# A split written into earlier products, two differences put first, and a second bank for the prompt's products, in an encoder layer on one core

## Chip, core and metric

The kernel runs on one core of a Trainium2 chip, as one launch. The metric is the device time of that core in microseconds (us). The core has five engines that run side by side, each working off its own instructions in order: TensorE (PE in the profile, its weight loads PEld) multiplies matrices into eight banks of PSUM, VectorE (DVE) and ScalarE (ACT) do the elementwise work, GpSimd (POOL) a part of it, and SyncE (SP) issues most DMAs. Engines wait for each other by semaphores.

## The reference

One encoder layer over two inputs: a sample of 1024 tokens and a prompt of 256, with a width of 1024, all in float32. Cut to what matters here:

```
h = rmsnorm(x, g_mix);  z = h @ w_in                       # queries, keys, values, gates
o_a = banded attention (8 heads);  o_b = dilated mixture (12 heads, merged to 4)
merged = gate_a * (o_a @ w_branch_a) + gate_b * (o_b @ w_branch_b)
x = x + merged @ w_out                                     # the output projection
h = rmsnorm(x, g_mlp)
x = x + square(relu(h @ w_up)) @ w_down                    # 1024 -> 4096 -> 1024
y = rmsnorm(x, g_final)
```

## The kernel before

**Products in parts.** A float32 product is made of three products of rounded numbers. Each operand is split into a high half (a copy to a rounded type, ScalarE, L185 in `split`) and a low half (the difference from it, VectorE, L186). One step in the contraction dimension is then three matmuls: high with low, low with high, high with high (`mm3` for the branches and the output projection, `six` for what follows). So each product waits for two operands that two engines make, one behind the other.

**Order of the stages.** The 1280 tokens are ten tiles of 128, in three blocks: 512 and 512 of the sample, 256 of the prompt (`BLOCKS`). After attention come the branch products (the loop over `jobs`, 48 products of 128 output columns each): for each block the eight of branch b and the first four of branch a, and after these, for each of the three blocks, the last four of branch a. A product's bank is multiplied by its gate (L1484) and added to `mT`, the merged rows turned over, one tile of `mT` for two or four column groups (L1485, both on VectorE). The last four products, of the 256-token block, are 256 wide; the eight ahead of them 512. The banks tagged "mm", three of them, are taken in turn.

Then comes the output projection, twice over all ten tiles, `hh` = 0 and 1 for the two halves of the output columns. `part(t)` splits a tile's merged rows: four copies and four low halves, two column groups each, into `mhi` and `mlo`; tile t + 2 is split after tile t's product. In the first half the result is added to the residual rows `x2` (L1599), which DMAs from SP bring (L1492). In the second half each tile is added (L1608), normed, turned over on TensorE (L340) and copied out (L1522, L1505), and the combinations for the next stage are made in between.

**Who sets the order.** From the end of attention to the end of the first half of the output projection a planner orders the instructions of each engine: it goes through the stretch with costs of its own and gives each engine the first instruction in the program that is ready. The place in the program is the priority. Most tiles there (`mT`, `x2`, `mhi`, `mlo`, gates, operands of the branches) come from one pool of 33 buffers of 4 KB a partition (`slot`). From the second half on (`manual_schedule` at L1579) each engine runs in the order of the program text.

**The up product.** It multiplies the sample's normed rows, as a 2 x 2 matrix of blocks, with the weights in Strassen's manner: seven block products instead of eight, named A11, A12, S2, S3, S1, A22, S4, with sums of blocks as operands. `combine` makes these sums (L1532 to L1537); `combine_last` makes the last of them, S4's operand, in two tiles, each a difference (L1545, in place) and its split. `up(j)` runs once for each of 16 pairs of column groups: the seven products into the banks x, y ("mm" and "pt") and z ("sc"), which add up over several products, so that a bank must be read before the next product adds to it. After S1, for instance, L1853 reads x on VectorE, and S4 adds to x later. The prompt's 256 rows are multiplied without the scheme, two products of 24 matmuls for a pair (`prompt(parts[0])` and `prompt(parts[3])`, L349), both in the one bank tagged "pv"; `prompt_out` reads such a bank on ScalarE (L1849 and L1850, relu and square, for both halves). In pair 0 the two stand next to each other, and pair 1's first follows at once; in the later pairs the first stands after A12, the second at the end. "sc" has two banks; z takes one for each pair, and in pair 0 the transposes of the last tile (`turn_prompt(9, ("pt", "sc"))`) the other.

Pair 0 takes extra steps between its products from `entering` in the last function: splits of S3, S1 and A22, `combine_last` after S3's product, `split_prompt` after A22's; and the first two products of pair 1 stand ahead of S4's. The operands of pair 1 are made on VectorE (L391, L314, L316); GpSimd adds the finished columns (L1925 to L1928), and SP stores them (L1930).

The down product that follows (`Down`) takes all eight banks in turn.

Of the kernel before, what the change touches and what calls it, by code (L numbers as in the profile page):

```python
# [11 lines left out]
F32R = mybir.dt.float32r  # L12
# [3 lines left out]
P = 128  # L16
D = 1024
KC = D // P
NS, NP = 1024, 256
T = NS + NP  # L20
NT = T // P
# [76 lines left out]
def encoder_kernel(  # L98
# [28 lines left out]
    def slot(name, shape=(P, D), dt=F32):  # L127
        return slots.tile(list(shape), dt, name=name, tag="m", bufs=N_M)
# [4 lines left out]
    def qslot(name, shape, dt=F32):  # L133
        return narrows[0].tile(list(shape), dt, name=name, tag="q", bufs=N_Q)

    def bank(tag, name=None):
        return psum.tile([P, 512], F32, name=name or tag, tag=tag, bufs={"mm": 3, "sc": 2, "pt": 2, "pv": 1}[tag])
# [46 lines left out]
    def split(hi, lo, src):  # L184
        nc.scalar.activation(hi, src, AF.Copy)  # L185
        nc.vector.tensor_tensor(lo, src, hi.bitcast(F32), op=ALU.subtract)  # L186
# [9 lines left out]
    def run(gen):  # L196
        for _ in gen:
            pass
# [146 lines left out]
    def six(ps, lefts, rights, first, last, mid=None):  # L345

        seq = [x for (lh, ll), (rh, rl) in zip(lefts, rights) for x in ((rl, lh), (rh, ll), (rh, lh))]
        for i, (a, b) in enumerate(seq):
            nc.tensor.matmul(ps, a, b, start=first and i == 0, stop=last and i == len(seq) - 1,  # L349
                             skip_group_check=True)  # L350
            if mid and i == len(seq) // 2 - 1:
                mid()

    def each(part, sub):
        hi, lo = part
        if sub is None:
            return [(hi[:, k, :], lo[:, k, :]) for k in range(KC)]
        if len(hi.shape) == 4:
            return [(hi[:, sub, k, :], lo[:, sub, k, :]) for k in range(4)]
        return [(hi[:, 4 * sub + k, :], lo[:, 4 * sub + k, :]) for k in range(4)]  # L360
# [4 lines left out]
    def prompt(part, tag="pv", mid=None):  # L365

        ps = bank(tag)
        lefts = [(hp[k // 4][0][:, k % 4, :], hp[k // 4][1][:, k % 4, :]) for k in range(KC)]
        six(ps[:, :NP], lefts, each(part, None), True, True, mid)
        return ps  # L370
# [937 lines left out]


    mT = Wide("mT", KC, F32, ())  # L1310
    if True:
        ob_hi, ob_lo = Wide("obhi", 2, F32R, ()), Wide("oblo", 2, F32R, ())
        o_hi, o_lo = Wide("ohi", 4, F32R, ()), Wide("olo", 4, F32R, ())
# [52 lines left out]
        n = len(order)  # L1366
# [49 lines left out]
        jobs = [(x, b, c) for b in range(3) for x in "ba" for c in range(KC if x == "b" else 4)]  # L1416
# [41 lines left out]
        for i, (x, b, c) in enumerate(jobs):  # L1458
            t0, n = BLOCKS[b]
            load_gate(i + 6)  # L1460
            if i in (0, 1, 2, 3, 8, 9):
                load_o(i + 4 if i < 4 else i)
            for f, t in side.get(i, ()):
                f(t)
            open_gate(i + 3)
            if i in (1, 4, 22, 26):
                fetch()
            elif i in (5, 8, 33, 35):
                w_as[(5, 8, 33, 35).index(i)] = weight(0)
            elif i in (38, 40, 42, 44):  # L1470
                prepare()
            hi, lo = w_bs[c // 4] if x == "b" else w_as[c // 2]
            per, src = (4, (ob_hi, ob_lo)) if x == "b" else (2, (o_hi, o_lo))
            cols = slice(P * (c % per), P * (c % per) + P)
            ps = bank("mm")
            run(mm3(ps[:, :n], [((hi[:, k, cols], lo[:, k, cols]), tuple(y.at(k, t0, n) for y in src))
                                for k in range(2 if x == "b" else 4)]))
            if (b, 0) not in mT.t:
                mT.block(b)
            m, sg = mT.at(c, t0, n), sgs.pop(i)  # L1480
            if x == "b":
                nc.vector.tensor_tensor(m, ps[:, :n], sg, op=ALU.mult)
            else:
                nc.vector.tensor_tensor(sg, ps[:, :n], sg, op=ALU.mult)  # L1484
                nc.vector.tensor_tensor(m, m, sg, op=ALU.add)  # L1485

    att_pool.close()

# [53 lines left out]
    def combine_last():  # L1542
        s2, a12 = combined[S2], combined[S4]
        for i in range(2):
            nc.vector.tensor_tensor(a12[i], a12[i], s2[i], op=ALU.subtract)  # L1545
            act[S4][i] = slot("chi", (P, 2, 512), F32R), slot("clo", (P, 2, 512), F32R)
            split(*act[S4][i], a12[i])

# [3 lines left out]
    with ExitStack() as pre:  # L1552
        late = pre.enter_context(tc.tile_pool(name="late", bufs=4))

        def lslot(name, shape=(P, D), dt=F32):
            return late.tile(list(shape), dt, name=name, tag="l4", bufs=6)

        for i in (4, 5, 6):
            specs[n_out + i] = specs[n_out + i][:2] + (lslot,)
        gm = slot("gm2")  # L1560
        nc.sync.dma_start(gm, g_mlp[0].partition_broadcast(P))
        xn = {}
        p0 = []
        b0 = right_up(0, p0, slot)

        def ahead():

            yield from b0
            yield from halves(A11, raws_h[0, 0])
            yield from halves(A12, raws_h[0, 1])  # L1570

        more, sums = ahead(), combine()
        for hh in range(2):
            sl = slice(512 * hh, 512 * hh + 512)
            ws = [weight(0) for _ in range(4)]
            parts = {}
            if hh:

                ctx.enter_context(tc.manual_schedule(engines=ALL))  # L1579

            def part(t):
                if t >= NT:
                    return
                n = 2 if hh else KC
                mhi = [qslot("mhi", (P, n, P), F32R) if hh else slot("mhi", (P, n, P), F32R) for _ in range(KC // n)]
                mlo = slot("mlo", (P, KC, P), F32R)
                for c in range(0, KC, 2):
                    split(mhi[c // n][:, c % n : c % n + 2, :], mlo[:, c : c + 2, :], mT.at(c, P * t, P, 2))
                parts[t] = [(mhi[k // n][:, k % n, :], mlo[:, k, :]) for k in range(KC)]

            part(0)
            part(1)
            for t in range(NT):
                m = parts.pop(t)
                ps = bank("mm")
                run(mm3(ps, [(m[k], (ws[k // 2][0][:, k % 2, :], ws[k // 2][1][:, k % 2, :]))
                             for k in range(KC)]))
                if hh == 0:
                    nc.vector.tensor_tensor(x2[t][:, sl], x2[t][:, sl], ps, op=ALU.add)  # L1599
                    part(t + 2)  # L1600
                    if 2 <= t < 6:
                        prepare()
                    elif t in (6, 7):
                        next(more)
                    continue
                turning = (turn_sample if t < 9 else turn_prompt)(t - 1) if t else iter(())
                next(turning, None)
                nc.vector.tensor_tensor(x2[t][:, sl], x2[t][:, sl], ps, op=ALU.add)  # L1608
                xn[t] = slot("xn", (P, D))
                ss = small.tile([P, 1], F32, name="ss")  # L1610
                nc.scalar.activation(xn[t], x2[t], AF.Square, accum_out=ss)
                sd = small.tile([P, 1], F32, name="sd")
                nc.scalar.activation(sd, ss, AF.Sqrt, bias=eps, scale=1.0 / D)
                if 0 < t < 7:
                    next(more)
                steps_of(sums, (0, 1, 4)[max(t - 7, 0)])
                rs = small.tile([P, 1], F32, name="rs")
                nc.vector.reciprocal(rs, sd)
                nc.vector.scalar_tensor_tensor(xn[t], x2[t], rs, gm, op0=ALU.mult, op1=ALU.mult)
                nc.sync.dma_start(scr_x[t], x2[t])  # L1620
                next(turning, None)
                part(t + 2)
                steps_of(more, (1, 1, 1, 1, 1, 3, 2, 0, 0, 0)[t])
                steps_of(sums, (2, 3)[t - 7] if 6 < t < 9 else 0)
        run(halves(S2, combined[S2]))
        run(sums)
# [215 lines left out]
    with ExitStack() as pre:  # L1842
# [25 lines left out]
        def up(j, b, parts, hooks):  # L1868
# [3 lines left out]
            def prompt_out(ps, dst):  # L1872
                for i, d in enumerate(dst):
                    relu2(d[:, 512:], ps[:, P * i : P * i + P])

            u = [stage(f"u{i}", TH) for i in range(7)]
            u11, u12, u22, u21 = u[A11], u[A12], u[A22], u[S3]
# [43 lines left out]
            if not j:  # L1921
                steps_of(nb, 4)
                prompt_out(prompt(parts[0]), (u11, u21))
            prompt_out(prompt(parts[3]), (u12, u22))
            nc.gpsimd.tensor_tensor(u[S1], u21, u22, op=ALU.add)  # L1925
            nc.gpsimd.tensor_tensor(u[S2], u[S1], u11, op=ALU.subtract)
            nc.gpsimd.tensor_tensor(u[S3], u11, u21, op=ALU.subtract)
# [52 lines left out]
```

## Time and profile before

| what | us |
|---|---|
| median of 3 runs | 1699.24 (1698.63 to 1699.45) |
| the profiled execution | 1699.29 |
| its span, first to last instruction | 1697.5 |
| TensorE busy | 1675.6 |
| VectorE busy | 951.2 |
| ScalarE busy | 720.1 |
| GpSimd busy | 511.7 |

The profile is of one execution. In its views a row is an instruction or a group of equal ones: start in us from the span's start, duration, engine, line, operation, what it writes and reads by the program's names, shapes, count, and in brackets how long the engine had stood idle before it and what ended that. A line of the waits names who waited, for whom, the time in all, how often, and the longest. A line of the windows has, for each engine, the busy time in that stretch and the count of instructions, and then the granted clock of TensorE, the DMA share and GB/s. Matmuls overlap: one that is shown with 0.39 us is followed by the next after 0.23, so the pace is read from the starts.

### The profile page before, as it was taken

Reading aid. Unit: us, or ns where it says so; the run is one execution under the profiler, and the core shown is the slowest. Engines: PE = TensorE matmul, PEld = TensorE weight load, DVE = VectorE, ACT = ScalarE, POOL = GpSimd, SP = SyncE. Lnnn points to the kernel's source line nnn. Section 1 sums busy time; section 2 is a strip of 40 time slices with the busy share of each in tenths; the row PEclk is TensorE's granted clock in tenths of the full one; section 3 lists DMA queues with packets and bytes.
Section 4 is the critical chain, followed back from the end, with each engine's and each line's share of the span. In section 5 each row is a group of like instructions: output and inputs, shape, how many; then the busy total and the mean of one; then the engine's idle time right before and its main releaser. Section 6 shows DMA issues by size and latency. Waiting matters only on the chain.

```text
span 1697.5 us, 24912 instructions
## 1 busy us (share of the span) xinstructions
PE 1675.6 (99%) x9268; PEld 1414.5 (83%) x9268; DVE 951.2 (56%) x1548; ACT 720.1 (42%) x1489; POOL 511.7 (30%) x404
## 2 busy tenths in 40 slices
PE   8999999999999999999999999999999999999998
PEld 7898888887778888888887888888887888888886
DVE  6732233445563565677278454545547777667575
ACT  6332323355552655654175333333334333333345
POOL 1312212212111472200100555546556332314150
PEclk9999999999999999999999999999999999999999
DMA  7417562576666893845121533443446845633333
GB/s 245 150 58 125 132 136 81 156 195 187 189 193 182 212 248 103 293 131 199 38 87 50 166 128 112 156 151 111 134 158 223 306 149 154 210 108 117 118 118 124
DMA packets 224410, 260.36 MB, mean 153 GB/s; under 512 B 29569, under 2 KB 154289, under 8 KB 224289
## 3 DMA queue, kind: packets, MB, share of 16 engines
q1 hardware_dynamic: 214976, 235.60, 43.9%
q0 software_dynamic: 7936, 20.54, 5.8%
q10 hardware_dynamic: 1376, 2.62, 0.4%
q8 instruction: 73, 1.20, 0.3%
q14 instruction: 49, 0.39, 0.1%
HBM read 173.03 MB, written 90.92 MB: 155 GB/s over the span
## 4 chain that ended last, share of the span: by engine, by line
PE 89%; DVE 4%; ACT 2%; DMA 2%; issue 2%; POOL 1%; SPq 0%; DVEq 0%; ACTq 0%; POOLq 0%
PE dn L349 20%; PE x L349 18%; PE mm L192 14%; PE z L349 9%; PE v L788 6%; PE mm L349 5%; PE pv L349 5%; PE y L349 4%; PE sc L538 1%; PE pv L1163 1%; PE pv L581 1%; PE pt L568 1%; PE pt L1148 1%; PE sc L1124 1%; PE tr L340 1%
## 5 line engine op out<-in xcount | busy, mean ns | idle before, releaser
L349 PE MATMUL dn<-dhi,ulo 128*128 128x512 f32 x448 | 174.6, 390 | 3.4 <-DVE ulo L186 3.4
L349 PE MATMUL dn<-dlo,uhi 128*128 128x512 f32 x448 | 174.3, 389 | 0.0
L349 PE MATMUL dn<-dhi,uhi 128*128 128x512 f32 x448 | 174.3, 389 | 0.0
L349 PE MATMUL x<-chi,wlo 128*128 128x512 f32 x424 | 167.5, 395 | 2.0 <-DVE u L1853 1.4
L349 PE MATMUL x<-clo,whi 128*128 128x512 f32 x424 | 165.8, 391 | 0.1
L349 PE MATMUL x<-chi,whi 128*128 128x512 f32 x424 | 165.1, 389 | 0.0
L316 DVE TENSOR_TENSOR wlo<-ta,whi 128x1024 fp32r<-128x1024 f32 x30 | 55.7, 1858 | 181.2 <-ACT whi L314 181.2
L316 DVE TENSOR_TENSOR wlo<-raw,whi 128x1024 fp32r<-128x1024 f32 x60 | 91.6, 1526 | 101.7 <-ACT whi L314 99.4
L391 POOL TENSOR_TENSOR tb<-raw 128x512 f32<-128x512 f32 x25 | 32.6, 1305 | 363.7 <-DMA raw<-in_w_in_dram 146.6
L349 PEld LDWEIGHTS dn<-dhi,ulo 128*128 128x128 f32 x448 | 84.1, 188 | 21.9 <-DVE ulo L186 4.5
L186 DVE TENSOR_TENSOR ulo<-uraw,uhi 128x1024 fp32r<-128x1024 f32 x56 | 93.3, 1686 | 11.6 <-ACT uhi L185 11.6
L349 PEld LDWEIGHTS dn<-dhi,uhi 128*128 128x128 f32 x448 | 84.1, 188 | 17.5
L349 PEld LDWEIGHTS dn<-dlo,uhi 128*128 128x128 f32 x448 | 84.1, 188 | 17.2
L349 PEld LDWEIGHTS x<-chi,wlo 128*128 128x128 f32 x424 | 79.8, 188 | 20.7 <-issue 3.4
L349 PEld LDWEIGHTS x<-chi,whi 128*128 128x128 f32 x424 | 79.6, 188 | 17.1
L349 PEld LDWEIGHTS x<-clo,whi 128*128 128x128 f32 x424 | 79.8, 188 | 14.7 <-DVE clo L316 0.4
L1678 POOL TENSOR_TENSOR t<-raw,t 128x1024 f32<-128x1024 f32 x16 | 46.9, 2948 | 142.1 <-DMA raw<-in_w_down_dram 142.1
L1832 DVE TENSOR_TENSOR v<-v,dn 128x512 f32<-128x512 f32 x90 | 59.5, 682 | 39.3 <-PE dn L349 34.9
L1925 POOL TENSOR_TENSOR u<-u,u 128x640 f32<-128x640 f32 x16 | 25.5, 1597 | 164.5 <-ACT u L1850 164.5
L558 ACT ACTIVATE s<-s,nm_b 128x128 f32<-128x128 f32 (+1 forms) x120 | 51.9, 434 | 54.5 <-DVE nm_b L550 54.5
L349 PE MATMUL pv<-phi,wlo 128*128 128x256 f32 x256 | 72.5, 283 | 1.7 <-ACT u L1849 1.7
L349 PE MATMUL dn<-dhi,up 128*128 128x512 f32 x224 | 73.5, 389 | 0.0
(318 smaller groups left out, 4646.5 us busy)
## 6 DMA issues: line engine op xcount, KB each, us to landing
scr_u<-u SPq DMA_DIRECT2D x112, 320.0 KB, 2.6
uraw<-scr_u SPq DMA_DIRECT2D x56, 512.0 KB, 4.4
raw<-in_w_in_dram SPq DMA_DIRECT2D x33, 512.0 KB, 5.6
raw<-in_w_up_dram SPq DMA_DIRECT2D x32, 512.0 KB, 5.4
raw<-in_w_down_dram SPq DMA_DIRECT2D x28, 512.0 KB, 6.6
sg<-scr_g SPq DMA_DIRECT2D x32, 256.0 KB, 6.1
uraw<-scr_u SPq DMA_DIRECT2D x28, 256.0 KB, 4.7
v<-scr_v SPq DMA_DIRECT2D x96, 64.0 KB, 2.7
```

The lines of the kernel that those rows point to most:

```text
L186: nc.vector.tensor_tensor(lo, src, hi.bitcast(F32), op=ALU.subtract)
L192: nc.tensor.matmul(ps, a, b, start=i == 0, stop=i == len(seq) - 1)
L316: nc.vector.tensor_tensor(lo, src, hi.bitcast(F32), op=ALU.subtract)
L340: nc.tensor.transpose(ps[:, P * i : P * (i + 1)], xn[t][:, P * k : P * (k + 1)], ident)
L349: nc.tensor.matmul(ps, a, b, start=first and i == 0, stop=last and i == len(seq) - 1, skip_group_check=True)
L391: (nc.vector if vector else nc.gpsimd).tensor_tensor(o, x, y, op=ALU.subtract)
L538: nc.tensor.matmul(at(k, h)[p0 : p0 + nq, :], qk[rows, p0 : p0 + nq], qk[rows, P + P * a : P + P * a + W], start=True, stop=True, skip_gro ...
L558: nc.scalar.activation(s[:, h, :W], s[:, h, :W], AF.Exp, bias=nm[:, h : h + 1], accum_out=l[:, h : h + 1])
L788: nc.tensor.matmul(ps[:, :n], a, b, start=k == 0 and j == 0, stop=k == KC - 1 and j == 2)
L1678: nc.gpsimd.tensor_tensor(o, a, b, op=ALU.subtract)
L1832: nc.vector.tensor_tensor(v, v, ps, op=ALU.add)
L1925: nc.gpsimd.tensor_tensor(u[S1], u21, u22, op=ALU.add)
```

## The change

Three edits. The split of a tile becomes a generator, `split_m`, that pauses after each two column groups. Tile 0 of the first half of the output projection is advanced by one such step behind each of the last five branch products (`i > len(jobs) - 6`), and `part(0)` is left out there; the second half calls it as before. In `combine_last` both differences stand ahead of both splits. And the second prompt product of each pair is written to a bank tagged "sc" instead of "pv".

```
--- before.py
+++ after.py
@@ -1308,6 +1308,19 @@
 
 
     mT = Wide("mT", KC, F32, ())
+
+    def split_m(t, hh, out):
+
+        n = 2 if hh else KC
+        mhi = [qslot("mhi", (P, n, P), F32R) if hh else slot("mhi", (P, n, P), F32R) for _ in range(KC // n)]
+        mlo = slot("mlo", (P, KC, P), F32R)
+        for c in range(0, KC, 2):
+            split(mhi[c // n][:, c % n : c % n + 2, :], mlo[:, c : c + 2, :], mT.at(c, P * t, P, 2))
+            yield
+        out += [(mhi[k // n][:, k % n, :], mlo[:, k, :]) for k in range(KC)]
+
+    first_m = []
+    early_m = split_m(0, 0, first_m)
     if True:
         ob_hi, ob_lo = Wide("obhi", 2, F32R, ()), Wide("oblo", 2, F32R, ())
         o_hi, o_lo = Wide("ohi", 4, F32R, ()), Wide("olo", 4, F32R, ())
@@ -1483,6 +1496,8 @@
             else:
                 nc.vector.tensor_tensor(sg, ps[:, :n], sg, op=ALU.mult)
                 nc.vector.tensor_tensor(m, m, sg, op=ALU.add)
+            if i > len(jobs) - 6:
+                next(early_m, None)
 
     att_pool.close()
 
@@ -1543,6 +1558,7 @@
         s2, a12 = combined[S2], combined[S4]
         for i in range(2):
             nc.vector.tensor_tensor(a12[i], a12[i], s2[i], op=ALU.subtract)
+        for i in range(2):
             act[S4][i] = slot("chi", (P, 2, 512), F32R), slot("clo", (P, 2, 512), F32R)
             split(*act[S4][i], a12[i])
 
@@ -1579,16 +1595,14 @@
                 ctx.enter_context(tc.manual_schedule(engines=ALL))
 
             def part(t):
-                if t >= NT:
-                    return
-                n = 2 if hh else KC
-                mhi = [qslot("mhi", (P, n, P), F32R) if hh else slot("mhi", (P, n, P), F32R) for _ in range(KC // n)]
-                mlo = slot("mlo", (P, KC, P), F32R)
-                for c in range(0, KC, 2):
-                    split(mhi[c // n][:, c % n : c % n + 2, :], mlo[:, c : c + 2, :], mT.at(c, P * t, P, 2))
-                parts[t] = [(mhi[k // n][:, k % n, :], mlo[:, k, :]) for k in range(KC)]
-
-            part(0)
+                if t < NT:
+                    parts[t] = []
+                    run(split_m(t, hh, parts[t]))
+
+            if hh:
+                part(0)
+            else:
+                parts[0] = first_m
             part(1)
             for t in range(NT):
                 m = parts.pop(t)
@@ -1921,7 +1935,7 @@
             if not j:
                 steps_of(nb, 4)
                 prompt_out(prompt(parts[0]), (u11, u21))
-            prompt_out(prompt(parts[3]), (u12, u22))
+            prompt_out(prompt(parts[3], "sc"), (u12, u22))
             nc.gpsimd.tensor_tensor(u[S1], u21, u22, op=ALU.add)
             nc.gpsimd.tensor_tensor(u[S2], u[S1], u11, op=ALU.subtract)
             nc.gpsimd.tensor_tensor(u[S3], u11, u21, op=ALU.subtract)
```

## The prediction

> **What bounds the kernel now.** I read the page's shares first, then what TensorE waited for over the whole span, then the timelines of the places the diff touches, engine by engine.
>
> ```profile
> PE 1675.6 (99%) x9268; PEld 1414.5 (83%) x9268; DVE 951.2 (56%) x1548; ACT 720.1 (42%) x1489; POOL 511.7 (30%) x404
> ```
>
> TensorE is busy 99% of the span. No product is added or removed, so the change can only give back idle time of TensorE: 1697.5 - 1675.6 = 21.9 us, the start of the program included. The waits of TensorE from 700 to 960 us, the stretch the diff touches, are these, longest first (time in all, count, longest; two smaller ones follow):
>
> ```profile
> PE pv L349 <- ACT u L1849: 1.7, 2, 0.9
> PE x L349 <- DVE u L1853: 1.4, 1, 1.4
> PE mm L192 <- DVE mlo L186: 1.3, 1, 1.3
> ```
>
> They are what the three edits aim at, 4.4 us together. The question is which of them are only handed on.
>
> **Edit 1: tile 0's split in the last products.** TensorE, then VectorE, at the end of the branch products:
>
> ```profile
> 781.98 0.28 PE L192 MATMUL mm<-ohi,whi 128*128 128x256 f32 x1
> 783.58 0.50 PE L192 MATMUL mm<-whi,mlo 128*128 128x512 f32 x1 [1.31 <-DVE mlo L186]
> 783.91 0.39 PE L192 MATMUL mm<-wlo,mhi 128*128 128x512 f32 x1
> 784.14 0.39 PE L192 MATMUL mm<-whi,mhi 128*128 128x512 f32 x1
> ...
> 779.24 1.22 DVE L235 TENSOR_TENSOR wlo<-raw,whi 128x1024 fp32r<-128x1024 f32 x1 [0.37 <-PE mm L192]
> 780.38 0.42 DVE L1484 TENSOR_TENSOR sg<-mm,sg 128x256 f32<-128x256 f32 x1
> ...
> 782.76 0.43 DVE L1485 TENSOR_TENSOR mT<-mT,sg 128x256 f32<-128x256 f32 x1
> 783.10 6.46 DVE L186 TENSOR_TENSOR mlo<-mT,mhi 128x256 fp32r<-128x256 f32 x19
> ```
>
> The output projection starts on the first low half (L186), which VectorE does only after the last gated sum (L1485): 19 low halves in a row, 6.46 / 19 = 0.34 us each. Nothing of tile 0 needs that sum: its columns belong to the first token block, whose last sum lies eight products earlier. The edit writes tile 0's four copies (ScalarE) and four low halves (VectorE), no DMA, into the last five products. There VectorE has room: with a low half a 256-wide product costs it 0.42 + 0.43 + 0.34 = 1.19 us, against 12 matmuls of 0.12 = 1.44 us on TensorE (the 0.12 is worked out under edit 3). With three banks a sum may be late by one product, so the 1.22 us weight split beside it (779.24) is covered too; without that cover it would cost the lateness once, at most 4 x 0.34 = 1.4 us, that is, the gain.
>
> The planner orders this stretch, and tile 0 now asks for its two buffers ahead of the residual rows (L1492), which move two buffers on; issued from 763.23, they are first used at 789.47, so this hides:
>
> ```profile
> 763.23 4.27 SPq L1492 DMA_DIRECT2D x<-in_x_sample_dram  x8
> ...
> 789.47 0.68 DVE L1599 TENSOR_TENSOR x<-x,mm 128x512 f32<-128x512 f32 x1
> ```
>
> Gain, by starts: the second matmul starts at 783.91; without a wait the first would start at 781.98 + 0.12 = 782.10 and the second 0.23 later, at 782.33. That is **1.58 us**. Bounds 0 and 1.58; I take 1.58. It is handed on to 926 us if nothing there keeps its own pace. VectorE's last wait for TensorE in that stretch is
>
> ```profile
> 874.53 0.69 DVE L1608 TENSOR_TENSOR x<-x,mm 128x512 f32<-128x512 f32 x1 [1.27 <-PE mm L192]
> ```
>
> and the saturated VectorE-ScalarE chain that follows starts from it, so it moves along.
>
> **Edit 2: differences ahead of the splits of S4.** VectorE, ScalarE, TensorE:
>
> ```profile
> 918.11 1.22 DVE L1545 TENSOR_TENSOR hraw<-hraw,s 128x1024 f32<-128x1024 f32 x1
> 920.51 1.23 DVE L186 TENSOR_TENSOR clo<-hraw,chi 128x1024 fp32r<-128x1024 f32 x1 [1.19 <-ACT chi L185]
> ...
> 924.06 1.22 DVE L186 TENSOR_TENSOR clo<-hraw,chi 128x1024 fp32r<-128x1024 f32 x1 [1.19 <-ACT chi L185]
> 925.20 0.68 DVE L1853 TENSOR_TENSOR u<-x,c 128x512 f32<-128x512 f32 x1
> ...
> 919.42 1.06 ACT L185 ACTIVATE chi<-hraw 128x1024 fp32r<-128x1024 f32 x1 [3.00 <-DVE hraw L1545]
> ...
> 924.26 0.39 PE L349 MATMUL y<-chi,whi 128*128 128x512 f32 x1
> 926.03 0.47 PE L349 MATMUL x<-chi,wlo 128*128 128x512 f32 x1 [1.38 <-DVE u L1853]
> 926.34 0.40 PE L349 MATMUL x<-clo,whi 128*128 128x512 f32 x1
> ```
>
> VectorE stands 1.19 us twice, waiting for ScalarE's copy. In the new order both differences stand first, at 918.11 and 1.15 later at 919.26; the first low half stays at 920.51; the second copy follows the first on ScalarE, from 920.5 to 921.6, so the second low half starts at 921.65 and ends by 922.9, and L1853 starts at 922.8 instead of 925.20 (neighbours overlap by about 0.08): 2.4 us earlier, done by 923.5. S4's product may not add to bank x before that read; TensorE is free for it at 924.26 + 0.23 = 924.49. So the wait goes whole, with 1.0 us to spare: 926.03 - 924.49 = 1.54, and the slow first matmul (0.31 instead of 0.23 to the next) 0.08: **1.62 us**. The bound below is 0, if another operand is late; none is, since S4's low halves are there at 922.9.
>
> **Edit 3: the second bank.** From here I follow three prompt products: column pair 0's two (call them A and B) and pair 1's first (C).
>
> ```profile
> 928.85 0.28 PE L349 MATMUL pv<-phi,wlo 128*128 128x256 f32 x1
> ...
> 929.35 0.28 PE L349 MATMUL pv<-phi,whi 128*128 128x256 f32 x1
> ...
> 931.86 0.28 PE L349 MATMUL pv<-phi,whi 128*128 128x256 f32 x1
> 933.01 0.39 PE L349 MATMUL pv<-phi,wlo 128*128 128x256 f32 x1 [0.87 <-ACT u L1849]
> ...
> 935.86 0.28 PE L349 MATMUL pv<-phi,whi 128*128 128x256 f32 x1
> 937.01 0.39 PE L349 MATMUL pv<-phi,wlo 128*128 128x256 f32 x1 [0.87 <-ACT u L1849]
> ...
> 939.87 0.28 PE L349 MATMUL pv<-phi,whi 128*128 128x256 f32 x1
> 940.09 0.50 PE L349 MATMUL x<-chi,wlo 128*128 128x512 f32 x1
> ...
> 946.36 0.47 PE L349 MATMUL x<-chi,wlo 128*128 128x512 f32 x1 [0.49 <-DVE wlo L316]
> ```
>
> The pace of 256-wide matmuls is (931.86 - 929.35) / 21 = 0.1195 us. A takes 931.86 - 928.85 = 3.01 us from its first start to its last, 0.26 more than 23 x 0.1195: its second matmul, the first with the prompt's low half, is late, and edit 2 brings that low half 2.4 us forward on VectorE. Without waits A starts twelve 512-wide matmuls after 924.49, 12 x 0.2275 (the pace of 783.91 to 784.14), at 927.22; B follows 24 x 0.1195 later, at 930.09, in its own bank, and its last matmul starts at 932.84 instead of 935.86. So edits 2 and 3 bring B's end **3.02 us** forward: 1.62, 0.26, and 1.14 for the bank between A and B.
>
> C's bank wait, 1.15 us from 935.86 to 937.01, is gone too, but I count nothing for it. What follows C does not hang on C, it hangs on B:
>
> ```profile
> 936.18 0.28 ACT L1849 ACTIVATE u<-pv 128x128 f32<-128x128 f32 x1 [2.88 <-PE pv L349]
> 937.21 1.04 ACT L314 ACTIVATE whi<-ta 128x1024 fp32r<-128x1024 f32 x1
> ...
> 938.28 1.75 DVE L316 TENSOR_TENSOR wlo<-ta,whi 128x1024 fp32r<-128x1024 f32 x1 [5.35 <-ACT whi L314]
> 943.03 0.69 DVE L1853 TENSOR_TENSOR u<-y,c 128x512 f32<-128x512 f32 x1 [2.99 <-POOL u L1927]
> ```
>
> ScalarE evicts B (936.18), then makes the high half of the next weights (937.21), VectorE the low half, done at 940.03, and the product after C starts at 940.09. Then GpSimd's sums of B's columns release L1853 at 943.03, behind which the low half for the product at 946.36 is queued. Both starts keep their distance from B's last matmul, 4.23 and 10.50 us. TensorE will run C at once and then stand 1.1 us for weights where it stood for a bank.
>
> The low half at 938.28 took 1.75 us, 0.53 more than the 1.22 of 918.11, with GpSimd at work beside it. The Trainium skill, "SBUF — State Buffer", section "Who interferes with whom", says that a VectorE instruction with two SBUF inputs contends with a GpSimd instruction that reads SBUF. By that rule the 0.53 goes only if the two no longer meet, and the sum below would be 1694.2; both start from B's eviction, in the same order as now, so I leave it in.
>
> In the later pairs the prompt products are far apart and TensorE waits for none, so nothing is gained. Sharing costs nothing either if a prompt product gets the bank of the prompt product before it. Should it get that of z, the last pair would pay:
>
> ```profile
> 1302.39 0.28 PE L349 MATMUL pv<-phi,wlo 128*128 128x256 f32 x1
> ...
> 1303.84 0.68 DVE L1853 TENSOR_TENSOR u<-z,c 128x512 f32<-128x512 f32 x1
> ```
>
> 1304.52 - 1302.39 = 2.1 us. I take 0: the pool's two banks are asked for in the order z, transposes, prompt, z, prompt, and so on, so in turn the prompt keeps to one of them and z to the other.
>
> **Sum.** The profiled execution took 1699.29 us, 1.79 more than its span; the median of the runs is 1699.24. 1699.29 - 1.58 - 3.02 = **1694.7 us**.
>
> **Rivals.**
> *The split stays late (0.12).* The planner grants buffers, and the copies of this stretch ran only when a buffer came free (the fence below). If VectorE's low halves still come behind the last sum, edit 1 gives 0: 1696.3.
>
> ```profile
> 772.56 1.34 ACT L185 ACTIVATE mhi<-mT 128x256 fp32r<-128x256 f32 x4 [2.84 <-DVE mT L1485]
> ```
>
> Against it: that buffer came free 10.5 us ahead of the first low half at 783.10, and VectorE stood idle in between (0.37 us at 779.24 alone).
> *The chain of 874 to 926 keeps its pace (0.08).* Then edit 1 is swallowed there: also 1696.3. Against it speaks the 1.27 us wait at 874.53.
> *C's wait is gained as well (0.05).* If the weights are not late, 1.1 more: 1693.6.
> *Slower (0.06).* The stretch from 874 to 926 has no slack and draws on the same buffers; tile 0 takes two of them earlier, so the tiles there get others. If a tile of that chain draws a buffer which a product still reads, it waits for up to one projection product, 24 x 0.23 = 5.5 us. One such wait eats the gain (1700.2), two make 1705.7; it decides from 8 us in sum. The profile shows no such wait now.
> *The clock (0.01).* A product at half clock would last 24 x 0.12 = 2.9 us longer; three of the 16 turned prompt products at half clock would outweigh the gain, all of them give 1741.
>
> ```profile
> 920.00:940.00 20.00, 16.88 (x105) 14.56 (x103) 12.74 (x14) 9.28 (x17) 2.54 (x2) 1.00 0.06 21
> ```
>
> The granted clock is 1.00 in the stretch with 3.1 us idle. The Trainium skill, "TensorE: Matmul & The Clock Gate", section "A second HAM failure mode: psum-queue depth-cycling", says that cycling through banks can make TensorE idle so often that its clock drops and recovers. This row disagrees: the banks x, pv and z change here already, at full clock.
>
> **How the numbers follow.** A measurement of this kernel tells about 0.2% from no change, 3.4 us, so below 1695.8 counts as faster. Forecast 0.68, at 1694.2 to 1695.3. Faster: 0.68 + 0.05 = 0.73. Within 0.2%: 0.12 + 0.08 = 0.20. Slower: 0.06 + 0.01 = 0.07. The range goes from 1693.6 (C gained) to 1696.8 (edit 1 lost, and another half microsecond, about one wait like that of 946.36).
>
> **What would show it.** Edit 1: TensorE's wait for mlo gone, four low halves ahead of the last L1485. Edit 2: two L1545 in a row, no 1.19 us waits, no wait of S4's product for L1853. Edit 3: no wait for L1849; instead a wait for wlo of about a microsecond after C and 0.8 us before the product that was at 946.36. It is wrong if mlo is still waited for, if the wait before S4 is replaced by one for its halves, or if a prompt product waits for z's read.

## The result and the profile after

The changed kernel takes **1694.91 us** (median of 10 runs, 1693.86 to 1695.48), the kernel before 1699.03 (10 runs beside it, 1698.54 to 1700.5): a ratio of **0.9971, 95% interval 0.9963 to 0.998**, faster by 0.2 to 0.4%. The prediction was 1694.7. The profiled execution took 1694.27 us with a span of 1692.5, against 1699.29 and 1697.5.

Lines have moved: L1484, L1485, L1545, L1599, L1608 are now L1497, L1498, L1560, L1613, L1622; the evictions L1849 and L1853 are L1863 and L1867, and GpSimd's sums L1925 to L1928 are L1939 to L1942. L185 to L349 are where they were.

The four longest waits of TensorE over the whole span, after (time in all, count, longest):

```profile
PE dn L349 <- DVE ulo L186: 3.1, 3, 1.6
PE x L349 <- DVE wlo L316: 1.6, 2, 1.1
PE warm L701 <- POOL ident masks.py:199: 1.4, 1, 1.4
PE tr L340 <- DVE xn L733: 1.1, 2, 0.9
```

All three waits that the edits aimed at are gone: for `mlo`, for the sum that reads x, and for the evictions of the prompt's bank. Between 780 and 960 us one has grown: `wlo` (L316), which was 0.5 us once, is 1.6 us in two. Waits that no edit touches vary from one execution to the next: that for `xn`, early in the program, is 2.3 us before and goes from 1.1 to 2.6 us over the kernels of this document.

**Edit 1**, TensorE and then VectorE at the end of the branch products:

```profile
781.83 0.28 PE L192 MATMUL mm<-ohi,whi 128*128 128x256 f32 x1
781.95 0.40 PE L192 MATMUL mm<-whi,mlo 128*128 128x512 f32 x1
782.18 0.40 PE L192 MATMUL mm<-wlo,mhi 128*128 128x512 f32 x1
...
767.99 0.42 DVE L186 TENSOR_TENSOR mlo<-mT,mhi 128x256 fp32r<-128x256 f32 x1
...
768.92 0.42 DVE L186 TENSOR_TENSOR mlo<-mT,mhi 128x256 fp32r<-128x256 f32 x1
...
769.86 0.75 DVE L186 TENSOR_TENSOR mlo<-mT,mhi 128x256 fp32r<-128x256 f32 x2
```

Tile 0's four low halves (the last row is two of them) are made at 768 to 771 us, 11 us ahead of their product, which follows the last branch product at the pace of the matmuls. From the last branch matmul to the second matmul of the projection it was 783.91 - 781.98 = 1.93 us, it is 782.18 - 781.83 = 0.35: 1.58 less.

**Edit 2**, VectorE, then TensorE around S4's product:

```profile
916.39 2.35 DVE L1560 TENSOR_TENSOR hraw<-hraw,s 128x1024 f32<-128x1024 f32 x2
918.80 2.36 DVE L186 TENSOR_TENSOR clo<-hraw,chi 128x1024 fp32r<-128x1024 f32 x2
921.08 0.68 DVE L1867 TENSOR_TENSOR u<-x,c 128x512 f32<-128x512 f32 x1
...
922.57 0.39 PE L349 MATMUL y<-chi,whi 128*128 128x512 f32 x1
922.80 0.39 PE L349 MATMUL x<-chi,wlo 128*128 128x512 f32 x1
923.03 0.39 PE L349 MATMUL x<-clo,whi 128*128 128x512 f32 x1
```

The two differences run as a pair, the two low halves as another, with no idle time in brackets, so the sum that reads x stands at 921.08 and is over a microsecond ahead of S4's product at 922.80, which starts 0.23 us behind the matmul before it.

**Edit 3**, TensorE at the ends of the three prompt products A, B and C, and at the products behind them; then ScalarE and VectorE, which make the weights:

```profile
928.27 0.28 PE L349 MATMUL pv<-phi,whi 128*128 128x256 f32 x1
928.39 0.28 PE L349 MATMUL sc<-phi,wlo 128*128 128x256 f32 x1
...
931.15 0.28 PE L349 MATMUL sc<-phi,whi 128*128 128x256 f32 x1
931.27 0.28 PE L349 MATMUL pv<-phi,wlo 128*128 128x256 f32 x1
...
934.03 0.28 PE L349 MATMUL pv<-phi,whi 128*128 128x256 f32 x1
935.40 0.50 PE L349 MATMUL x<-chi,wlo 128*128 128x512 f32 x1 [1.09 <-DVE wlo L316]
...
941.66 0.47 PE L349 MATMUL x<-chi,wlo 128*128 128x512 f32 x1 [0.51 <-DVE wlo L316]
...
931.47 0.28 ACT L1863 ACTIVATE u<-sc 128x128 f32<-128x128 f32 x1 [1.75 <-PE sc L349]
...
932.51 1.04 ACT L314 ACTIVATE whi<-ta 128x1024 fp32r<-128x1024 f32 x1
...
933.58 1.76 DVE L316 TENSOR_TENSOR wlo<-ta,whi 128x1024 fp32r<-128x1024 f32 x1 [4.77 <-ACT whi L314]
938.32 0.69 DVE L1867 TENSOR_TENSOR u<-y,c 128x512 f32<-128x512 f32 x1 [2.98 <-POOL u L1941]
...
940.30 1.21 DVE L316 TENSOR_TENSOR wlo<-tb,whi 128x1024 fp32r<-128x1024 f32 x1
```

A, B and C follow each other 0.12 us apart. Then TensorE stands, from 934.03 to 935.40, because the low half of `ta`, the operand of the product after C, is only ready at 933.58 + 1.76 = 935.34: ScalarE evicts B (931.47) before it makes the high half (932.51). The idle time has moved from C's bank to the weights behind it.

### The profile page after: what moved, and what is told of

It is laid out like the page before. It is cut to its first block, busy times and chain, and to the rows that moved or that the text cites. A ratio compares the mean times of both kernels' runs of the same rounds, so it can differ in the third digit from the quotient of the medians.

```text
span 1692.5 us, 24900 instructions
## 1 busy us (share of the span) xinstructions
PE 1675.2 (99%) x9268; PEld 1415.3 (84%) x9268; DVE 953.4 (56%) x1548; ACT 719.6 (43%) x1489; POOL 513.1 (30%) x404
## 4 chain that ended last, share of the span: by engine, by line
PE 92%; DVE 3%; ACT 2%; DMA 1%; issue 1%; POOL 0%; SPq 0%; DVEq 0%; ACTq 0%
PE dn L349 20%; PE x L349 19%; PE mm L192 14%; PE z L349 9%; PE v L788 6%; PE mm L349 5%; PE y L349 5%; PE sc L349 3%; PE pv L349 3%; PE sc L538 1%; PE pv L1163 1%; PE pv L581 1%; PE pt L568 1%; PE pt L1148 1%; PE sc L1124 1%
## 5 line engine op out<-in xcount | busy, mean ns | idle before, releaser
L349 PE MATMUL dn<-dhi,ulo 128*128 128x512 f32 x448 | 174.6, 390 | 3.1 <-DVE ulo L186 3.1
L349 PE MATMUL dn<-dhi,uhi 128*128 128x512 f32 x448 | 174.3, 389 | 0.0
L349 PE MATMUL dn<-dlo,uhi 128*128 128x512 f32 x448 | 174.3, 389 | 0.0
L349 PE MATMUL x<-chi,wlo 128*128 128x512 f32 x424 | 167.4, 395 | 1.7 <-DVE wlo L316 1.6
L349 PE MATMUL x<-clo,whi 128*128 128x512 f32 x424 | 165.8, 391 | 0.1
L349 PE MATMUL x<-chi,whi 128*128 128x512 f32 x424 | 165.1, 389 | 0.0
L316 DVE TENSOR_TENSOR wlo<-ta,whi 128x1024 fp32r<-128x1024 f32 x30 | 55.8, 1859 | 180.4 <-ACT whi L314 180.4
L316 DVE TENSOR_TENSOR wlo<-raw,whi 128x1024 fp32r<-128x1024 f32 x60 | 91.3, 1522 | 101.1 <-ACT whi L314 101.1
L349 PEld LDWEIGHTS dn<-dhi,ulo 128*128 128x128 f32 x448 | 84.1, 188 | 21.6 <-DVE ulo L186 4.3
L349 PEld LDWEIGHTS dn<-dhi,uhi 128*128 128x128 f32 x448 | 84.1, 188 | 17.5
L349 PEld LDWEIGHTS dn<-dlo,uhi 128*128 128x128 f32 x448 | 84.1, 188 | 17.4
L349 PEld LDWEIGHTS x<-chi,wlo 128*128 128x128 f32 x424 | 79.8, 188 | 20.0 <-issue 1.7
L349 PEld LDWEIGHTS x<-chi,whi 128*128 128x128 f32 x424 | 79.6, 188 | 17.0
L349 PEld LDWEIGHTS x<-clo,whi 128*128 128x128 f32 x424 | 79.8, 188 | 14.9 <-DVE clo L316 0.4
L349 PE MATMUL dn<-dhi,up 128*128 128x512 f32 x224 | 73.5, 389 | 0.0
L1939 POOL TENSOR_TENSOR u<-u,u 128x640 f32<-128x640 f32 x16 | 25.6, 1597 | 156.5 <-ACT u L1864 156.5
L349 PE MATMUL z<-chi,wlo 128*128 128x512 f32 x184 | 72.1, 392 | 0.0
```

## Experiments

Single times of one kernel scatter by 1 to 3 us, and the gains are of 1 to 2 us. So beside each time stands a distance in the trace: from **M1**, the second matmul of the output projection, to **M2**, the first matmul of pair 1's S1 product (the row at 946.36 before, 941.66 after). Edits 2 and 3 lie between the two, edit 1 ahead of both. M1 and M2 come from one profiled execution of each kernel, the medians from 5 to 11 runs of each.

| kernel | median us | ratio to before, 95% interval | M1 | M2 | M2 - M1 |
|---|---|---|---|---|---|
| before | 1699.03 | | 783.91 | 946.36 | 162.45 |
| changed | 1694.91 | 0.9971 (0.9963 to 0.998) | 782.18 | 941.66 | 159.48 |
| e1_split_only | 1697.41 | 0.9988 (0.9979 to 0.9997) | 782.19 | 944.66 | 162.47 |
| e2_differences_only | 1696.83 | 0.9987 (0.9979 to 0.9996) | 783.37 | 943.96 | 160.59 |
| e3_bank_only | 1698.0 | 0.9994 (0.9985 to 1.0003) | 783.35 | 944.74 | 161.39 |
| e4_bank_first_pair | 1694.66 | 0.9971 (0.996 to 0.9981) | 782.53 | 941.98 | 159.45 |
| e5_weights_early | 1692.07 | 0.9959 (0.9945 to 0.9972) | 782.99 | 940.41 | 157.42 |
| e6_weights_half_early | 1692.38 | 0.9962 (0.9949 to 0.9974) | 782.93 | 940.35 | 157.42 |
| e7_c_waits_again | 1695.08 | 0.9975 (0.9966 to 0.9983) | 783.16 | 942.61 | 159.45 |
| e8_weights_early_one_bank | 1694.94 | 0.9975 (0.9965 to 0.9984) | 781.82 | 941.50 | 159.68 |
| e9_c_waits_for_b | 1694.29 | 0.9972 (0.9962 to 0.9983) | 782.63 | 942.14 | 159.51 |
| e10_c_waits_weights_early | 1693.29 | 0.9967 (0.9954 to 0.998) | 781.95 | 940.72 | 158.77 |

The theory: each edit gives what its own step says, the gains are handed on, and C's bank wait is worth nothing, since what follows C hangs on weights made behind B's eviction. The rival to the last point: each wait of TensorE is worth its own length.

### Each edit alone

Edit 1 alone is the changed kernel with edits 2 and 3 taken back:

```
         for i in range(2):
             nc.vector.tensor_tensor(a12[i], a12[i], s2[i], op=ALU.subtract)
-        for i in range(2):
             act[S4][i] = slot("chi", (P, 2, 512), F32R), slot("clo", (P, 2, 512), F32R)
...
-            prompt_out(prompt(parts[3], "sc"), (u12, u22))
+            prompt_out(prompt(parts[3]), (u12, u22))
```

> Edit 1 alone: tile 0's split in the last branch products; S4's differences and both prompt products as before. Theory (the gain of 1.58 us is made at 782 us and handed on through the chain of 874 to 926 us): 1697.5 us in all, 1.6 under before; the output projection's second matmul starts 1.6 to 1.7 us earlier, and S4's wait for L1853 and the two bank waits for L1849 stay as long as they were (1.4, 0.9, 0.8). Rival (the chain keeps its own pace): 1699.1, VectorE's last wait for TensorE near 874 us grows or one in the chain appears, and the wait of S4's product is 1.6 longer.

1.62 us under before by the medians, and M2 - M1 is before's to 0.02: nothing of the 1.58 is swallowed between 782 and 945 us. Its waits for S4's sum (1.4) and for the bank (twice 0.9) are as long as before's. Theory held.

Edit 2 alone is the kernel before with the line `for i in range(2):` put between the difference and its split:

> Edit 2 alone: S4's two differences ahead of its two splits; tile 0's split and the prompt products as before. Theory: 1697.2 us, that is 1.62 for S4's product and 0.26 for the prompt's low half under before; the two bank waits for L1849 stay at 0.8 to 0.9. Rival (another operand of S4's product is late, or the prompt's bank takes the time back): 1699.1, or anything over 1698.3.

M2 - M1 shrinks by 162.45 - 160.59 = 1.86, against 1.62 + 0.26 = 1.88; the median by 2.2. The two bank waits are there, 0.87 each. Theory held.

Edit 3 alone is the kernel before with `"sc"` in the second prompt product:

> Edit 3 alone: the second prompt product in the other bank. Theory (what follows C, pair 1's first prompt product, hangs on the eviction of B, pair 0's second): 1697.9 us, 1.14 under before; C's bank wait turns into a wait for wlo (L316) of about 1.1 us ahead of the product after C. Rival (each bank wait is worth its own length): 1696.8, 2.3 under before, with no wait for wlo there.

The distance shrinks by 1.06, the median by 1.03: one bank wait, not two. Its TensorE rows behind C:

```profile
938.48 0.50 PE L349 MATMUL x<-chi,wlo 128*128 128x512 f32 x1 [1.09 <-DVE wlo L316]
...
944.74 0.47 PE L349 MATMUL x<-chi,wlo 128*128 128x512 f32 x1 [0.51 <-DVE wlo L316]
```

The wait for `wlo` stands where the bank wait stood. The interval of the ratio reaches past 1, so this small gain rests on the trace, not on the times.

### The bank in the later pairs

```
-            prompt_out(prompt(parts[3], "sc"), (u12, u22))
+            prompt_out(prompt(parts[3], "pv" if j else "sc"), (u12, u22))
```

> The changed kernel with the other bank for pair 0's second prompt product alone; the later pairs' stay in the first bank. Theory (the later pairs neither gain nor pay): 1694.9 us, the changed kernel's time within 0.3. Rival (the alternation matters in the 14 later pairs, or costs a wait behind z there): different by over 0.5 us, with a wait of a prompt product for an eviction in the one of the two and not in the other.

1694.66 beside 1694.91, and the same distance (159.45). The later pairs neither gain nor pay; neither trace shows a wait of TensorE between 945 and 1300 us.

### The weights made earlier

If the product after C hangs on weights that stand behind B's eviction, then making them ahead of it must give the rest. Pair 1's next two operands, four steps of their generator, are moved between the two evictions:

```
                 steps_of(nb, 4)
                 prompt_out(prompt(parts[0]), (u11, u21))
+                steps_of(nb, 4)
             prompt_out(prompt(parts[3], "sc"), (u12, u22))
```

> The changed kernel, and pair 1's last two weight halves of ta and tb (L314, L316) made between A's eviction and B's, four steps earlier in program order. Theory (after the change the product after C hangs on those low halves, which stand behind B's eviction, and TensorE has nothing else late there): the product after C follows C's last matmul without a wait (1.25 us by starts), the product that was at 941.66 is not late either (0.67 by starts), 1.9 in all: 1693.0 us. Rival (the time is taken by the next wait, for u's sums on GpSimd or a bank): 1694.9, with a wait of a product for L1867 or an eviction in place of those for L316.

1692.07 us, and 2.06 us less from M1 to M2. ScalarE, VectorE, TensorE at the end of C, and GpSimd's first sum (one line further down here):

```profile
930.42 1.04 ACT L314 ACTIVATE whi<-ta 128x1024 fp32r<-128x1024 f32 x1
931.37 1.04 ACT L314 ACTIVATE whi<-tb 128x1024 fp32r<-128x1024 f32 x1
932.32 0.25 ACT L1863 ACTIVATE u<-sc 128x128 f32<-128x128 f32 x1
...
931.50 1.23 DVE L316 TENSOR_TENSOR wlo<-ta,whi 128x1024 fp32r<-128x1024 f32 x1 [1.86 <-ACT whi L314]
932.64 1.22 DVE L316 TENSOR_TENSOR wlo<-tb,whi 128x1024 fp32r<-128x1024 f32 x1
...
934.82 0.28 PE L349 MATMUL pv<-phi,whi 128*128 128x256 f32 x1
934.94 0.40 PE L349 MATMUL x<-chi,wlo 128*128 128x512 f32 x1
...
933.50 1.79 POOL L1940 TENSOR_TENSOR u<-u,u 128x640 f32<-128x640 f32 x1 [107.67 <-ACT u L1864]
```

ScalarE had stood idle while B ran; now it makes both high halves there, B's eviction (932.32) still starts 0.38 us behind B's last matmul (931.94) against 0.32 in the changed kernel, and the product after C follows C's last matmul 0.12 us behind. No wait of TensorE for `wlo` is left. The gain closes by starts: the first gap was 935.40 - 934.03 - 0.12 = 1.25, the second 941.66 - 935.40 - 24 x 0.2275 = 0.80, in all 2.05. The theory held; its 1.9 had read the second gap from the last matmul of z (941.66 - 940.76 - 0.23 = 0.67) and left out that the product behind a wait starts slowly.

The same with two steps, `ta` alone (`steps_of(nb, 2)`):

> The same with ta's two halves alone made early (two steps). Theory (the product that was at 941.66 hangs on tb's low half, which stands behind L1867, released by GpSimd's sums after B's eviction, whatever starts before): the first wait of 1.1 us goes and the second grows from 0.5 to about 1.7, so nothing is gained: 1694.9. Rival (each wait is worth its own length): 1693.7.

Neither came true: 1692.38 us and the same distance as with four, 157.42. My theory forgot that the generator goes on from where it stands: with `ta` done early, the next step pair of pair 1 is `tb`'s, and it moves into the place that `ta` had, ahead of the sum that waits for GpSimd. VectorE of this kernel:

```profile
934.32 1.75 DVE L316 TENSOR_TENSOR wlo<-tb,whi 128x1024 fp32r<-128x1024 f32 x1 [1.65 <-ACT whi L314]
939.05 0.69 DVE L1867 TENSOR_TENSOR u<-y,c 128x512 f32<-128x512 f32 x1 [2.98 <-POOL u L1942]
```

`tb`'s low half is there at 936.07, for a product at 940.35; in the changed kernel it stood behind that sum and was done at 941.51. So one step pair is enough, and the run told nothing apart between the two theories.

### C's bank wait put back

The first try put C into the second bank and left B there:

```
-                pa = prompt(parts[0])
+                pa = prompt(parts[0], "sc" if j == 1 else "pv")
...
-            prompt_out(prompt(parts[3], "sc"), (u12, u22))
+            prompt_out(prompt(parts[3], "pv" if j == 1 else "sc"), (u12, u22))
```

> The changed kernel with C, pair 1's first prompt product, in the bank that B just used, so that it waits for B's eviction again; pair 1's second prompt product in the bank C leaves, the later pairs as in the changed kernel. Theory (C's bank wait is free, since the product after it hangs on B): C starts about 1.15 us later by starts, with a wait of 0.9 for the eviction, the wait for wlo after it shrinks from 1.1 to about nothing, and the time stays: 1694.9 us. Rival (C's wait is worth its length): 1696.0.

The time is 1695.08, but the run is inconclusive: C did not wait. C's first matmul follows B's last by 0.12 us (932.11 to 932.23), ahead of B's eviction at 932.43, so C is not in B's bank. Between B and C pair 1's z asks for one of the two banks of that tag and keeps it past C, so z must have B's and C the other; the waits of 1.1 and 0.5 us for `wlo` are as in the changed kernel. The second try gives A the second bank and B the first, so that C follows B in one bank:

```
-                prompt_out(prompt(parts[0]), (u11, u21))
-            prompt_out(prompt(parts[3], "sc"), (u12, u22))
+                prompt_out(prompt(parts[0], "sc"), (u11, u21))
+            prompt_out(prompt(parts[3], "sc" if j else "pv"), (u12, u22))
```

> The changed kernel with A in the second bank and B in the first, so that A and B do not meet and C, pair 1's first prompt product, follows B in the same bank; the later pairs as in the changed kernel. Theory (C's bank wait is free, since the product after C hangs on low halves that follow B's eviction): C's first matmul waits 0.9 for the eviction, 1.15 by starts, the wait for L316 after C is gone or nearly so, and the time stays at 1694.9 us. Rival (C's wait is worth its length): 1696.0.

TensorE of this kernel:

```profile
932.79 0.38 PE L349 MATMUL pv<-phi,wlo 128*128 128x256 f32 x1 [0.87 <-ACT u L1863]
...
935.64 0.28 PE L349 MATMUL pv<-phi,whi 128*128 128x256 f32 x1
935.88 0.50 PE L349 MATMUL x<-chi,wlo 128*128 128x512 f32 x1
942.14 0.47 PE L349 MATMUL x<-chi,wlo 128*128 128x512 f32 x1 [0.51 <-DVE wlo L316]
```

C waits 0.87 us, the product after it starts 0.24 us behind C's last matmul, only 0.12 late, and the distance is 159.51 beside 159.48, the median 1694.29 beside 1694.91. A microsecond of waiting at C costs 0.03 us, less than such distances scatter. That is the prediction's point by itself. Now the same banks with the early weights of above (`steps_of(nb, 4)` behind A's eviction):

> The same banks as in the run before, with ta's and tb's halves made between the evictions of A and B as in the kernel of early weights (1692.1 us). Theory (with the weights there, nothing lies over C's wait any more, so the same wait now costs its length): 1693.2 us, C's wait of 0.9 is the only one left between S4 and the end of pair 1. Rival (C's wait is free in any case, or the gain of the early weights had another source): 1692.1.

1693.29 us against 1692.07 without C's wait, and 158.77 - 157.42 = 1.35 us by the distance. The same wait that was free now costs its length, and 0.2 more than the 1.15 expected. TensorE at the end of B and the start of C:

```profile
931.08 0.28 PE L349 MATMUL pv<-phi,whi 128*128 128x256 f32 x1
932.27 0.39 PE L349 MATMUL pv<-phi,wlo 128*128 128x256 f32 x1 [0.91 <-ACT u L1863]
```

By starts C is 932.27 - 931.08 - 0.12 = 1.07 us late, and its slow first matmul adds 0.10 (the second starts at 932.49): 1.17, the length that was expected. The other 0.18 do not lie at C: from M1 to B's last matmul it is 149.13 us here and 931.94 - 782.99 = 148.95 without C's wait. They come in the second half of the output projection: from the transposes of its first tile to those of its eighth it is 891.59 - 847.03 = 44.56 us here and 892.40 - 848.07 = 44.33 without C's wait, with no wait of TensorE in between and a granted clock of 1.00 in both. What slowed the matmuls there the traces don't show.

### Early weights with one bank

The early weights, with edits 1 and 2 alone:

```
+                steps_of(nb, 4)
-            prompt_out(prompt(parts[3], "sc"), (u12, u22))
+            prompt_out(prompt(parts[3]), (u12, u22))
```

> The early weights without edit 3: edits 1 and 2, all prompt products in one bank, ta's and tb's halves between A's eviction and B's. Theory (C's bank wait of 1.15 and the wait for the weights lie over each other, so each alone hides the other): the two bank waits of 0.8 to 0.9 are there, the waits for wlo are gone, and against the changed kernel 1.14 is lost between A and B and at most 0.7 won at the product that was at 941.66: 1695.4 us. Rival (the two waits add up): 1694.1, as far under the kernel without edit 3 (1696.0) as the early weights take off the changed kernel (1.9).

Nearer the theory than the rival. The two bank waits are there (0.87 each) and the waits for `wlo` are gone; the distance is 159.68, 0.20 over the changed kernel, where 1.14 - 0.7 = 0.44 was expected. The 0.7 was the second gap, which is 0.80, and C's bank wait of 1.13 (1.03 by starts and 0.10 for the slow first matmul) replaces a wait of 1.25: 1.13 + 1.13 - 1.25 - 0.80 = 0.21. Taken as a square of M2 - M1:

| | weights behind B's eviction | weights ahead of it |
|---|---|---|
| prompt products in one bank | 160.59 (e2) | 159.68 (e8) |
| B in the other bank (edit 3) | 159.48 (changed) | 157.42 (e5) |

(e2 stands for edits 1 and 2 together, as edit 1 leaves the distance alone.) Edit 3 is worth 1.11 us with the weights late and 2.26, both bank waits, with the weights early; the early weights are worth 0.91 with one bank and 2.06 with two. The two waits lie over each other, and each edit alone leaves the other to end last.

The kernel of early weights has the lowest median: 1692.07 us, a ratio of 0.9959 (0.9945 to 0.9972) to before. Its distance is 2.06 us under the changed kernel's; the two were not timed side by side, and the intervals of their ratios overlap.

## Why the prediction was right

*The sum.* 162.45 - 159.48 = 2.97 us between the marks, against 3.02 for edits 2 and 3; 1.58 at edit 1, as worked out. The medians differ by 4.12 us, 0.5 less than the sum of 4.60, and the profiled pair by 5.02, 0.4 more. Of its 5.0 us of span 0.15 lie ahead of edit 1 (781.98 to 781.83) and 1697.5 - 946.36 - (1692.5 - 941.66) = 0.30 behind M2; over the other kernels the time behind M2 goes from 750.48 to 751.45 whatever the edit, so that part is scatter of single executions.

*Edit 1, "Against it: that buffer came free 10.5 us ahead".* Right: the planner put the low halves at 768 to 771 us, earlier than the prediction needed. They lie ahead of the last five products (the gate of the first of these is at 776.39), so the room that the prediction reckoned for VectorE inside these products was not put to the test. "The chain of 874 to 926 keeps its pace" fell by e1; in the changed kernel VectorE's wait at the start of that chain is still 1.27 us:

```profile
872.82 0.69 DVE L1622 TENSOR_TENSOR x<-x,mm 128x512 f32<-128x512 f32 x1 [1.27 <-PE mm L192]
```

*Edit 2.* Counted from the shift at M1 (1.73), S4's product should start at 924.49 - 1.73 = 922.76 and A at 925.49; they start at 922.80 and 925.52. The 0.26 for the prompt's low half came too: A takes 928.27 - 925.52 = 2.75 us.

*Edit 3, "C's bank wait is gone too, but I count nothing for it".* Right, and shown alone by e9. The distances from B's last matmul, predicted to stay at 4.23 and 10.50, are 935.40 - 931.15 = 4.25 and 941.66 - 931.15 = 10.51. The foretold waits came: 1.09 and, by starts, 0.80 us; the row of the second shows 0.51, since matmuls overlap.

*The low half that took 1.75 us.* It takes 1.76 after, as it was left in the sum. GpSimd's sums beside it:

```profile
932.68 1.58 POOL L1939 TENSOR_TENSOR u<-u,u 128x640 f32<-128x640 f32 x1 [107.67 <-ACT u L1864]
934.34 2.43 POOL L1940 TENSOR_TENSOR u<-u,u 128x640 f32<-128x640 f32 x1
936.73 1.56 POOL L1941 TENSOR_TENSOR u<-u,u 128x640 f32<-128x640 f32 x1
```

With the early weights, where that low half ends (931.50 + 1.23 = 932.73) ahead of GpSimd's first sum (933.50), it takes 1.23. This is the contention that the Trainium skill, "SBUF — State Buffer", section "Who interferes with whom", describes for a VectorE instruction with two SBUF inputs and a GpSimd instruction that reads SBUF. In these rows the one that starts second pays. The low half starts at 933.58, 0.68 us before the first sum ends (934.26), and takes 1.76 - 1.23 = 0.53 longer; the first sum, with 1.58, is as short as the third, beside which VectorE stands idle. The second sum starts at 934.34, 1.00 before the low half ends (935.34), and takes 2.43 - 1.56 = 0.87 longer. So the later one loses the overlap but for 0.13 to 0.15 us: it nearly stands still.

*Later pairs.* Nothing gained or paid (e4), and the last pair's second prompt product starts at 1297.68 without a wait, ahead of z's read at 1298.84. The outcome is as forecast, the ground for it is not: the prediction let z and the prompt keep to one bank each in turn, and e7 shows pair 1's z in the bank that B had left. By what rule the banks were given out no trace shows. *Slower by buffers* did not occur, nor did the clock drop:

```profile
918.00:938.00 20.00, 18.91 (x117) 16.95 (x117) 12.31 (x14) 9.59 (x17) 5.24 (x3) 1.00 0.15 58
```

Here a bank changes for each prompt product, and the granted clock is 1.00.

## What to carry to other kernels

A wait is worth its length only if nothing else ends at the same place: before counting a wait as gain, look for the operand of the *next* product, ask from which event it starts, and keep its distance from that event. Two waits that cover each other are told apart by a square of four kernels; here the early weights were worth 0.91 us alone and 2.06 with the second bank. For gains below the scatter of the times, measure between two marks in the trace on either side of the edit: the distances of the four kernels that should agree lie between 159.45 and 159.51, where single times of one kernel lie 1 to 3 us apart. One kernel (e10) shows that such a distance can be off by 0.2 us for no reason that the trace names.

## What the runs showed of the hardware

The first matmul behind a wait costs about 0.1 us more than the wait: 0.50 instead of 0.39 in its row, and the next starts 0.33 behind it instead of 0.23 (935.40 to 935.73, the second start as the trace has it). It does not take a microsecond of idle time: in e9 the product after C is only 0.12 us late (935.88), and its row and the next start (936.21) show the same 0.50 and 0.33. So a gap read from the bracket (1.09) is short of the gap by starts (1.25), and a gain worked out from starts closes where one from brackets does not.
